# Gate matrix of a PEER layer: written as outer products by TensorE instead of scattered by GpSimd, with tiles 3 to 6 dense

## The chip, the cores and the metric

One core of a Trainium2 chip runs one decoder layer in float32. The metric is the device time of one execution in microseconds (us). TensorE is called PE here, VectorE DVE, ScalarE ACT, GpSimd POOL and SyncE SP; "PEld" is the weight load of PE.

## What is computed

The layer has a mixer (mLSTM heads beside stick-breaking attention), a cross-attention into 256 memory tokens, and a PEER feed-forward. Only the last part changes. For each of 1024 tokens, 8 heads pick 16 experts out of 16384; each expert is one row of `u` and one row of `v`, 1024 wide:

```
s_top, i_top = lax.top_k(s, PEER_TOPK)                    # per half of the product key
cand     = s_top[:, :, 0, :, None] + s_top[:, :, 1, None, :]
cand_idx = i_top[:, :, 0, :, None] * PEER_N_KEYS + i_top[:, :, 1, None, :]
best, pos = lax.top_k(cand..., PEER_TOPK)                 # 16 experts of a token and head
gates = softmax(best)
act = gelu(einsum('cd,ced->ce', xb, u[eb])) * gb          # eb: 128 experts of a token
y   = einsum('ce,ced->cd', act, v[eb])
```

An expert's number e is 128 i + p: i is one of 128 blocks of 128 experts, p the place in the block.

## The kernel before

The 1024 tokens are eight tiles of 128. The front of the kernel takes them in groups of (1, 2, 2, 1, 2) tiles: `part_a` (norm and projections), `mixers`, `post` (output projection, cross-attention, `route` with the expert scores) and `topk`, which finds a tile's 128 experts and gates per token. Work of the next group fills in beside the current one (`fill`). After `topk` there are two ways to compute the feed-forward:

- **Sparse tiles** (0, 1, 6, 7 before): `experts(tb)`. POOL fetches one row of `u` or `v` per token with an indirect DMA (L777, 512 KB), 128 of each per tile, into five buffers `uv`. DVE multiplies and sums a `u` row (L784) or adds a scaled `v` row to `y` (L790 for the first, L792). Four sparse tiles make 1024 gathers, and DVE has one instruction for each (a second, short one reads the accumulator).
- **Dense tiles** (2, 3, 4, 5 before): `dense()`. All 16384 experts are computed for the four tiles' N = 512 tokens, in 128 blocks. Block i needs a product h (24 matmuls, L850 in `hmat`), a GELU, a multiplication by block i of the gate matrix G (L876), a split into a high and a low half, and a product with `v` (24 matmuls, L896). Seven accumulators `y` stand in PSUM, the eighth, `y8`, is summed by DVE. `hmat` runs ahead of the gates by up to `ring` blocks.

G has 16384 rows and 512 columns and is zero but for 128 entries per token. It lies in HBM (`G_scr`). `zero_fill` (L116) first writes zeros in 256 DMAs on SP's queue, five after each weight load. Then, for each dense tile, `topk` issues 128 indirect DMAs on POOL (L748), each adding 128 gates of four bytes at places listed in `idx`. `dense` reads G block by block on SP's queue (L875).

The order on each engine is fixed when the program is built: a scheduler simulates the program and writes one list per engine. Each engine takes its own list strictly in order; an instruction that waits holds up all behind it. `dense` stands after the front in the program, and PE's part of it keeps that order.

Of the kernel before, what the change touches and what calls it, by code (L numbers as in the profile page):

```python
# [26 lines left out]
C_ID, C_TRI, C_MU, C_ST, C_IO, C_TK, C_SN, C_END = 0, 128, 256, 384, 512, 512 + NCAND, 520 + NCAND, 648 + NCAND  # L27


def constants():  # L30
    c = np.zeros((128, C_END), np.float32)
    p = np.arange(128)[:, None]
    f = np.arange(128)[None, :]
    c[:, C_ID:C_ID + 128] = p == f
    c[:, C_TRI:C_TRI + 128] = -(p >= f).astype(np.float32)
    c[:, C_MU:C_MU + 128] = np.where(p <= f, 0.0, NEG)
    c[:, C_ST:C_ST + 128] = p < f
    c[:, C_SN:C_SN + 128] = np.where(p < f, 0.0, NEG)
    c[:, C_IO:C_IO + NCAND] = np.arange(NCAND)[None, :]
    c[:, C_TK:C_TK + 8] = p + 128 * np.arange(8)[None, :]  # L40
    return c


class Layer:
# [65 lines left out]
    def zero_fill(self):  # L110
        z = self.fp.tile([128, 1, 128], F32, name="zero", bufs=1)
        self.nc.vector.memset(z, 0.0)
        n = self.zn
        g = self.G_d.rearrange("(c p n f) o -> c p n (f o)", p=128, n=n, f=128)
        for i in range(g.shape[0]):
            self.tc.keep_in_program_order(self.nc.sync.dma_start(g[i], z.to_broadcast([128, n, 128])))  # L116
            yield

# [30 lines left out]
    def ksmall(self, shape, name, bufs=2, dt=F32):  # L149
        return self.gp.tile(shape, dt, name=name, bufs=bufs)  # L150

    def xs(self):
        return self.fp.tile([128, D], F32, name="xs", bufs=3)
# [64 lines left out]
    def wload(self, w, c0):  # L218
        W = []
        for i in range(2):  # L220
            t = self.wtile([128, 4, 256])
            self.nc.sync.dma_start(t, w[512 * i:512 * i + 512, c0:c0 + 256].rearrange("(k p) n -> p k n", p=128))
            W += [t[:, k, :] for k in range(4)]
        for _ in range(self.zrate):
            next(self.zeros, None)
        return W
# [44 lines left out]
    def setup(self):  # L271
# [22 lines left out]
    def part_a(self, t0, nt):  # L294
# [13 lines left out]
        def ev_k(j, b):  # L308
            kc = self.mp.tile([128, T], F32, name="tk", bufs=2)
# [4 lines left out]
        def ev_v(t, b):  # L314
            vc = self.mp.tile([128, 512], F32, name="tk", bufs=2)
# [366 lines left out]
    def topk(self, tb, top, ti):  # L682
# [27 lines left out]
        pf = self.ksmall([128, NH, K16], "kpf", 1)  # L710
# [11 lines left out]
        self.idx[tb] = self.gp.tile([128, 128], I32, name="idx", bufs=4)  # L722
        self.gate[tb] = self.gp.tile([128, 128], F32, name="gate", bufs=4)
        exf = ex.rearrange("p h k -> p (h k)")
        if self.is_dense(tb):
            j = self.dl.index(tb)
            V.tensor_scalar(self.idx[tb], exf, float(128 * self.nd), self.c[:, C_TK + j:C_TK + j + 1],
                            op0=OP.mult, op1=OP.add)
        else:
            V.tensor_copy(self.idx[tb], exf)  # L730
        g = self.gate[tb].rearrange("p (h k) -> p h k", h=NH)
# [8 lines left out]
        rows = slice(128 * tb, 128 * tb + 128)  # L740
        self.dump("idx", self.idx[tb], lambda d: d[rows])
        self.dump("gate", self.gate[tb], lambda d: d[rows])
        if self.is_dense(tb):
            all_ = []
            for h in range(NH):
                same = []
                for k in range(16 * h, 16 * h + 16):
                    d = nc.gpsimd.indirect_dma_start(  # L748
                        out=self.G_d, out_offset=bass.IndirectOffsetOnAxis(ap=self.idx[tb][:, k:k + 1], axis=0),
                        in_=self.gate[tb][:, k:k + 1], in_offset=None, compute_op=OP.add)  # L750
                    for e in same:
                        self.tc.declare_no_dep(d.ins, e.ins, reason="one head's experts differ")
                    same.append(d)
                    if self.xt:
                        for e in self.scat[-self.xt:]:
                            self.tc.declare_no_dep(d.ins, e.ins, reason="tiles' columns differ")
                all_ += same
            self.scat += all_
# [56 lines left out]
    def dense_head(self):  # L815
# [4 lines left out]
        self.dh = f(tc.tile_pool(name="dh", bufs=1, side="right"))  # L820
# [36 lines left out]
    def dense(self):  # L857
# [3 lines left out]
        Gv = self.G_d.rearrange("(i p t) o -> i p (t o)", i=128, p=128)  # L861
# [8 lines left out]
        def gpart(i):  # L870
# [58 lines left out]
    def build(self, experts=True):  # L929
# [52 lines left out]
        for _ in self.zeros:  # L982
            pass
        self.front_ctx.close()
        tc = self.tc
        if self.nd:
            with tc.tile_pool(name="dp", bufs=1) as self.dp:
# [31 lines left out]
GROUPS = (1, 2, 2, 1, 2)  # L1019
# [18 lines left out]
```

## Time and profile before

| | us |
|---|---|
| median of 3 runs | 3686.97 |
| lowest and highest run | 3682.38, 3691.51 |
| the profiled execution: its span | 3682.8 |
| PE busy | 3024.6 (82%) |
| DVE busy | 2442.9 (66%) |
| POOL busy | 2135.7 (58%) |
| ACT busy | 1108.1 (30%) |

The span is the time of the one profiled execution, from its first instruction to its last. Shares of a whole span say little in this kernel, because its stages have different limits. A table by stretches of time shows for each stretch how long each engine was busy, the clock granted to PE (1.00 is 2.4 GHz), the busy share of the 16 DMA engines and the rate that they moved. A table of waits names who waited, for whom, for how long.

### The profile page before, as it was taken

The page shows a single profiled execution, that of the slowest core. Times are in us where ns is not written, and L with a number is a line of the kernel's source. Part 1 is how long each engine was busy: PE and PEld are TensorE (multiplying, and loading weights), DVE is VectorE, ACT ScalarE, POOL GpSimd, SP SyncE. Part 2 cuts the span into 40 slices and gives each one's busy share as a digit, 9 for nine tenths or more (in the row PEclk, how much of TensorE's full clock was granted, in tenths as well). Part 3 has the DMA queues.
Part 4 walks back from the last instruction along what each step waited for, and adds up shares of the span by engine and source line. Part 5 has one row for each costly group of instructions (what it writes and reads, how often), then busy time and mean ns, then how long its engine had stood idle before and what let it go on. Part 6 is the DMA issues. An engine that isn't in the chain of part 4 may idle for free.

```text
span 3682.8 us, 41986 instructions
## 1 busy us (share of the span) xinstructions
PE 3024.6 (82%) x14232; PEld 2481.8 (67%) x14232; DVE 2442.9 (66%) x5088; ACT 1108.1 (30%) x2236; POOL 2135.7 (58%) x1540
## 2 busy tenths in 40 slices
PE   8989999978975656664655655999999999999995
PEld 7777877767765545553444544777888887888884
DVE  0217767799953564435422265999888888888888
ACT  3423434323521212222222212233233233332323
POOL 0000545563368888888888887545555555555554
PEclk9999999989987878886787877999999999999997
DMA  9997999999895757664484656989999999999998
GB/s 295 281 322 239 350 334 343 364 316 330 284 304 130 212 139 182 181 154 103 78 216 104 178 118 179 351 309 344 344 342 343 346 339 327 347 340 345 337 334 297
DMA packets 572592, 992.49 MB, mean 269 GB/s; under 512 B 114392, under 2 KB 370520, under 8 KB 572376
## 3 DMA queue, kind: packets, MB, share of 16 engines
q0 software_dynamic: 221184, 537.23, 45.2%
q1 hardware_dynamic: 332144, 418.62, 34.9%
q10 hardware_dynamic: 19048, 33.96, 2.6%
q8 instruction: 112, 1.84, 0.2%
q14 instruction: 104, 0.85, 0.1%
HBM read 939.04 MB, written 50.59 MB: 269 GB/s over the span
## 4 chain that ended last, share of the span: by engine, by line
PE 25%; POOL 12%; issue 7%; DMA 5%; DVE 3%; ACT 1%; POOLq 0%; DVEq 0%; ACTq 0%
PE h L850 12%; PE y L896 11%; POOL G_scr L748 9%; POOL uv L777 4%; DMA uv<-v_in,idx 2%; PE h L896 2%; DMA G_scr<-gate,idx 1%; DMA uv<-u_in,idx 1%; DVE y L792 1%; DVE uv L784 0%; DVE vl L836 0%; DVE al L880 0%; ACT L123 0%; DVE y L899 0%; DVE ge L876 0%
## 5 line engine op out<-in xcount | busy, mean ns | idle before, releaser
L777 POOL DMA_INDIRECT uv<-u_in,idx x512 | 646.1, 1262 | 879.2 <-DVE idx L730 367.1
L748 POOL DMA_INDIRECT G_scr<-gate,idx x512 | 846.8, 1654 | 156.2 <-issue 151.3
L777 POOL DMA_INDIRECT uv<-v_in,idx x512 | 642.6, 1255 | 491.8 <-DVE act L784 224.3
L792 DVE SCALAR_TENSOR_TENSOR y<-uv,act,y 128x1024 f32<-128x1024 f32 x508 | 651.0, 1282 | 341.6 <-DMA uv<-v_in,idx 339.6
L784 DVE CUSTOM_DVE_ANT_0 uv<-uv,xf 128x1024 f32<-128x1024 f32 x512 | 623.8, 1221 | 367.8 <-DMA uv<-u_in,idx 367.0
L850 PE MATMUL h<-xs,uh 128*128 128x512 f32 x1968 | 619.5, 396 | 33.4 <-DVE y L899 15.3
L850 PEld LDWEIGHTS h<-xs,uh 128*128 128x128 f32 x1968 | 373.2, 190 | 120.0 <-DVE y L899 20.8
L238 PE MATMUL ps<-b,w 128*128 128x256 f32 (+1 forms) x2048 | 406.8, 356 | 32.3 <-ACT pq L670 18.3
L238 PEld LDWEIGHTS ps<-b,w 128*128 128x128 f32 x2048 | 347.7, 201 | 76.9 <-ACT pq L670 19.4
L850 PE MATMUL h<-xs,ul 128*128 128x512 f32 x984 | 388.7, 395 | 7.7 <-DVE ul L836 7.7
L896 PE MATMUL y<-vh,ah 128*128 128x512 f32 x896 | 352.3, 393 | 25.8 <-ACT ah L878 22.7
L834 ACT CAST uh<-ur 128x1024 fp32r<-128x1024 f32 x128 | 134.6, 1052 | 760.8 <-PE h L850 644.5
L896 PE MATMUL y<-vh,al 128*128 128x512 f32 x896 | 352.0, 393 | 1.0 <-DVE al L880 1.0
L896 PE MATMUL y<-vl,ah 128*128 128x512 f32 x896 | 350.3, 391 | 2.2 <-DVE vl L836 2.2
L238 PE MATMUL ps<-hT,w 128*128 128x256 f32 (+1 forms) x1280 | 254.8, 354 | 38.4 <-issue 16.9
L238 PEld LDWEIGHTS ps<-hT,w 128*128 128x128 f32 x1280 | 215.6, 201 | 68.7 <-issue 19.7
L850 PEld LDWEIGHTS h<-xs,ul 128*128 128x128 f32 x984 | 187.6, 191 | 48.4 <-DVE ul L836 8.1
L896 PEld LDWEIGHTS y<-vh,ah 128*128 128x128 f32 x896 | 169.3, 189 | 61.8 <-ACT ah L878 23.1
L250 PE MATMUL ps<-w,hT 128*128 128x256 f32 x768 | 184.8, 395 | 19.7 <-DMA w<-w_in_in 19.2
L836 DVE TENSOR_TENSOR ul<-ur,uh 128x1024 fp32r<-128x1024 f32 x128 | 156.6, 1223 | 63.7 <-ACT uh L834 63.7
L896 PEld LDWEIGHTS y<-vl,ah 128*128 128x128 f32 x896 | 169.2, 189 | 40.2 <-DVE vl L836 3.1
L896 PEld LDWEIGHTS y<-vh,al 128*128 128x128 f32 x896 | 169.1, 189 | 38.8 <-DVE al L880 1.7
(269 smaller groups left out, 4269.9 us busy)
## 6 DMA issues: line engine op xcount, KB each, us to landing
w<-w_in_in SPq DMA_DIRECT2D x140, 512.0 KB, 5.8
ur<-uT_in SPq DMA_DIRECT2D x128, 512.0 KB, 6.2
vr<-v_in SPq DMA_DIRECT2D x128, 512.0 KB, 5.9
w<-peer_wq_in SPq DMA_DIRECT2D x80, 512.0 KB, 5.4
G_scr<-zero SPq DMA_DIRECT2D x256, 128.0 KB, 4.9
G<-G_scr SPq DMA_DIRECT2D x128, 256.0 KB, 6.7
w<-w_out_in SPq DMA_DIRECT2D x40, 512.0 KB, 5.9
w<-wq_in SPq DMA_DIRECT2D x40, 512.0 KB, 5.8
```

The costliest lines, as they stand in the source:

```text
L238: nc.tensor.matmul(b[:, :T], W[k][:, 128 * (j % 2):128 * (j % 2) + 128], hT[:, k, :T], start=k == 0, stop=k == KC - 1)
L250: nc.tensor.matmul(b[:, 256 * q:256 * q + 256], hT[:, k, 128 * t:128 * t + 128], W[q][k], start=k == 0, stop=k == KC - 1)
L748: d = nc.gpsimd.indirect_dma_start(out=self.G_d, out_offset=bass.IndirectOffsetOnAxis(ap=self.idx[tb][:, k:k + 1], axis=0), in_=self.gate[ ...
L777: nc.gpsimd.indirect_dma_start(out=g, out_offset=None, in_=A[tbl], in_offset=bass.IndirectOffsetOnAxis(ap=self.idx[tb][:, s:s + 1], axis=0))
L784: V.tensor_tensor_reduce(u, u, xf, op0=OP.mult, op1=OP.add, scale=1.0, scalar=0.0, accum_out=act[:, s:s + 1])
L792: V.scalar_tensor_tensor(y, v, act[:, k:k + 1], y, op0=OP.mult, op1=OP.add)
L834: self.nc.scalar.copy(hi, src)
L836: self.nc.vector.tensor_sub(lo, src, hi.bitcast(F32))
L850: nc.tensor.matmul(h[:, :N], a[:, ks], self.xs_[:, x, k, :], start=n == 0, stop=n == 3 * KC - 1)
L896: nc.tensor.matmul(b, a[x][:, ts], v[w][:, qs], start=m == 0 and (j == 0 if acc else i == 0), stop=m == 2 and (j == 127 if acc else i == n ...
```

## The change

- `zero_fill`, `idx` of the dense tiles and the 512 indirect DMAs are gone. In their place `topk` calls `spread` for a dense tile. It transposes expert numbers and gates, so that a token is a column. For each token ACT writes |n - p| (L754) and, for two tokens at once, relu(1 - |n - p|) (L757): a one-hot of the place p of each of its 128 experts. DVE writes a one-hot of the block i times the gate (L755). PE multiplies the two (L760): a 128 x 128 slice of G. ACT copies four tokens' slices from PSUM in two halves (L763) and, after 16 tokens, stores two 512 KB pieces (L766) on its own queue. The staging buffers `gs` are two, one per half.
- `dense` reads G eight blocks at a time (2 MB, in runs of 512 bytes), 16 DMAs in all instead of 128.
- The groups are (1, 2, 2, 2, 1) and the dense tiles 3, 4, 5, 6, so 0, 1, 2 and 7 are sparse. Buffers are smaller: `ring` 5 for 12, `stb` 4 for 5, `wb` 5 for 6, `xs` 2 for 3, `tk` 1 for 2. Two pools wait tile by tile for their memory (`reuse_waits="tile"`).

On POOL, before, the 16 scatters of a head stand between gathers of tile 1 and later tiles:

```order
L777 DMA uv<-v_in,idx 128x1024 x33
L777 DMA uv<-u_in,idx 128x1024 x27
L748 DMA G_scr<-gate,idx 8388608x1 x16
L777 DMA uv<-u_in,idx 128x1024 x5
L748 DMA G_scr<-gate,idx 8388608x1 x16
```

Of such groups there are 32. Now POOL's list holds the 1024 gathers and nothing else.

On DVE, before, the first multiplication of dense gates (L876) stands amid gathers of tile 1 (L784, L792) and the choice of experts of the last group (L717 to L720); 441 gathers are consumed ahead of it:

```order
L720 TENSOR_REDUCE kex<-kA 128x8
L876 TENSOR_TENSOR ge<-ge,G 128x512 x2
L792 SCALAR_TENSOR_TENSOR y<-uv,act,y 128x1024
L717 TENSOR_TENSOR kA<-consts,kpf 128x400
L880 TENSOR_TENSOR al<-ge,ah 128x512 x2
L784 ISA uv,act<-uv,xf 128x1024
```

In the changed kernel the same multiplication (L885) comes when the experts of tile 7, the last, are chosen (L707 to L717):

```order
L705 TENSOR_TENSOR kA<-consts,kpos 128x400
L707 TENSOR_TENSOR kA<-kA,kcidx 128x400
L708 TENSOR_REDUCE kex<-kA 128x8
L717 CAST idx<-kex 128x128
L875 MEMSET y_13675 128x512
L885 TENSOR_TENSOR ge<-ge,G 128x512 x4
L844 TENSOR_TENSOR ul<-ur,uh 128x1024
L889 TENSOR_TENSOR al<-ge,ah 128x512
L885 TENSOR_TENSOR ge<-ge,G 128x512
L792 ISA uv,act<-uv,xf 128x1024
```

All 768 gathers of tiles 0, 1 and 2 are consumed ahead of it, and none of tile 7. Between the last of the 768 and this place DVE's list holds what tiles 5 and 6 need for their slices of G, and tile 7's `post` and `topk`.

On PE, at the end of the slices of tiles 5 and 6 (L760), the list now goes:

```order
L858 MATMUL h<-xs,ul 128x512
L734 MATMUL pt<-consts,kex 128x128
L735 MATMUL pt<-consts,kbest 128x128
L760 MATMUL pt<-ab 128x128 x126
L760 MATMUL pt<-ab 128x128 x128
L188 MATMUL pt<-consts,xs 128x128 x4
L760 MATMUL pt<-ab 128x128 x2
L228 MATMUL ps<-b_12893,w 128x128 x6
```

L228 on `b_12893` is the query projection of tile 7's cross-attention: it and all behind it, up to the dense blocks, come after the last slices. Tiles 3 and 4 have such a row of slices too, earlier. Four of the 128 products h stand ahead of the first product with `v`; before, there were twelve.

The core of the diff:

```diff
-GROUPS = (1, 2, 2, 1, 2)
+GROUPS = (1, 2, 2, 2, 1)
-        Layer(ctx, tc, A, out[0], S, GROUPS, dense=(2, 3, 4, 5), uvb=5, stb=5, wb=6, ..., ring=12, ...
+        Layer(ctx, tc, A, out[0], S, GROUPS, dense=(3, 4, 5, 6), uvb=5, stb=4, wb=5, ..., ring=5, ...
...
-        if self.is_dense(tb):
-            all_ = []
-            for h in range(NH):
-                same = []
-                for k in range(16 * h, 16 * h + 16):
-                    d = nc.gpsimd.indirect_dma_start(
-                        out=self.G_d, out_offset=bass.IndirectOffsetOnAxis(ap=self.idx[tb][:, k:k + 1], axis=0),
-                        in_=self.gate[tb][:, k:k + 1], in_offset=None, compute_op=OP.add)
...
+        if dense:
+            yield from self.spread(self.dl.index(tb), exf, gate)
+
+    def spread(self, j, exf, gate):
...
+        for c in range(128 // TC):
+            st = [self.ksmall([128, 64, TC], "gs", 2) for _ in range(2)]
+            for q in range(TC // 4):
+                b = self.bank("pt")
+                for m in range(2):
+                    ab = self.ksmall([128, 2, 2, 128], "ab", 2)
+                    for i in range(2):
+                        t = TC * c + 4 * q + 2 * m + i
+                        nc.scalar.activation(ab[:, 0, i, :], iota, AF.Abs, bias=sl[:, 0, t:t + 1])
+                        V.tensor_scalar(ab[:, 1, i, :], iota, sl[:, 1, t:t + 1], sl[:, 2, t:t + 1], op0=OP.is_equal,
+                                        op1=OP.mult)
+                    nc.scalar.activation(ab[:, 0], ab[:, 0], AF.Relu, scale=-1.0, bias=self.one)
+                    for i in range(2):
+                        o = 128 * (2 * m + i)
+                        nc.tensor.matmul(b[:, o:o + 128], ab[:, 0, i, :], ab[:, 1, i, :], start=True, stop=True)
+                bv = b.rearrange("p (t h i) -> p t h i", t=4, h=2)
+                for h in range(2):
+                    nc.scalar.copy(st[h][:, :, 4 * q:4 * q + 4].rearrange("p i t -> p t i"), bv[:, :, h, :])
+                yield
+            for h in range(2):
+                nc.scalar.dma_start(self.G_d[:, h, (128 // TC) * j + c], st[h])
...
-            G = dp.tile([128, N], F32, name="G", bufs=self.gb)
-            nc.sync.dma_start(G, Gv[i])
-            V.tensor_mul(ge, ge, G)
+            if i % NB == 0:
+                self.Gt = dp.tile([128, N // TC, NB, TC], F32, name="G", bufs=self.gb)
+                nc.sync.dma_start(self.Gt, self.G_d[:, i // 64, :, i % 64:i % 64 + NB, :])
+            gv = ge.rearrange("p (c t) -> p c t", t=TC)
+            V.tensor_mul(gv, gv, self.Gt[:, :, i % NB, :])
```

## Rows read from the trace of the kernel before

**Rows 1.** By stretches: length; busy per engine (instructions); PE clock, DMA share, GB/s.

```profile
0.00:365.00 365.00, 322.12 (x1829) 277.95 (x1830) 109.35 (x455) 123.17 (x351) 0.20 (x4) 0.97 0.94 287
365.00:990.00 625.00, 566.97 (x2891) 464.99 (x2890) 509.10 (x1213) 249.93 (x605) 306.64 (x257) 0.95 0.94 334
990.00:1055.00 65.00, 55.92 (x274) 44.49 (x273) 55.64 (x118) 22.10 (x55) 28.96 (x26) 0.92 0.86 299
1055.00:2277.00 1222.00, 729.74 (x3386) 590.16 (x3384) 544.83 (x1768) 284.12 (x652) 1014.53 (x676) 0.78 0.62 153
2510.00:2760.00 250.00, 248.48 (x1089) 203.87 (x1088) 220.25 (x286) 76.04 (x96) 145.43 (x108) 1.00 0.95 345
```

**Rows 2.** Waits in 1055 to 2270 us: who and for whom, total us, times, longest.

```profile
POOL G_scr L748 <- issue: 151.3, 496, 0.3
DVE y L792 <- DMA uv<-v_in,idx: 279.1, 33, 23.2
DVE uv L784 <- DMA uv<-u_in,idx: 272.6, 39, 25.0
```

**Rows 3.** Groups by line on POOL: count, busy us, mean ns, idle before them.

```profile
L748 POOL DMA_INDIRECT G_scr<-gate,idx x512 | 846.8, 1654 | 156.2 <-issue 151.3 <-DMA G_scr<-gate,idx 4.6 <-DVE kA L686 0.3
```

**Rows 4.** Dense lines: first and last start; busy by stretch; pieces of the chain.

```profile
L896 PE MATMUL y<-vh,ah x896: 388/389/796, 2277.1 to 3648.0; 128*128 128x512 f32 x180
...
1880.00:2277.00 397.00, 80.31 (x288) 60.67 (x288) 0.78 0.59 143
...
2515.28 5.47 PE h L850 x24
```

**Rows 5.** DMA queues in 365 to 990 us, then in 0 to 365: packets, MB, share.

```profile
q0 software_dynamic: 36864, 134.23, 58.8%
q1 hardware_dynamic: 64120, 66.64, 31.7%
...
q1 hardware_dynamic: 133522, 98.94, 89.8%
```

**Rows 6.** DMA queues of the whole span, and issues: count, KB each, us to landing.

```profile
q1 hardware_dynamic: 332144, 418.62, 34.9%
q10 hardware_dynamic: 19048, 33.96, 2.6%
...
x_scr<-xa ACTq DMA_DIRECT2D x3, 1024.0 KB, 7.2
```

**Rows 7.** DVE in order of time near 950 us: start, length.

```profile
949.29 1.28 DVE L792 SCALAR_TENSOR_TENSOR y<-uv,act,y 128x1024 f32<-128x1024 f32 x1
950.49 0.69 DVE L533 SCALAR_TENSOR_TENSOR sq<-pz,sq 128x512 f32<-128x512 f32 x1
```

**Rows 8.** Groups by line and shape, rows like the new instructions on ACT and DVE.

```profile
L128 ACT ACTIVATE ta<-ta 128x128 f32<-128x128 f32 x16 | 4.9, 308 | 30.3 <-DVE ta L354 30.2
L129 ACT ACTIVATE ta<-ta,one 128x128 f32<-128x128 f32 x16 | 6.4, 401 | 0.2
L128 ACT ACTIVATE ta<-ta 128x256 f32<-128x256 f32 x24 | 9.9, 412 | 27.0 <-DVE ta L354 27.0
L129 ACT ACTIVATE ta<-ta,one 128x256 f32<-128x256 f32 x24 | 12.1, 505 | 0.2
L658 ACT COPY ta<-pt 128x256 f32<-128x256 f32 x64 | 23.1, 374 | 189.8 <-DVE kti L665 94.2 <-PE pt L655 91.3 <-DVE kti L662 3.9
L424 DVE TENSOR_SCALAR mnM<-mM 4x128 f32<-4x128 f32 x8 | 1.7, 213 | 0.2
```

**Rows 9.** Tile 0 alone, 0 to 420 us: query projection, scores, choice of experts.

```profile
L584 ACT ACTIVATE b<-ps x8: 277/278/278, 201.6 to 214.7; 128x128 f32<-128x128 f32 x8
...
L658 ACT COPY ta<-pt x8: 372/375/378, 268.6 to 312.1; 128x256 f32<-128x256 f32 x8
...
L720 DVE TENSOR_REDUCE kex<-kA x16: 559/569/570, 325.2 to 366.1; 128x8 f32<-128x400 f32 x16
```

More of the change, by code (lines that the diff above doesn't have):

```diff
@@ L108, in row_bcast @@
         self.nc.scalar.dma_start(dst, bass.AP(tensor=r.tensor, offset=r.offset, ap=[[0, 128], [1, D]]))
[L110 to L117, printed above, removed]
     def is_dense(self, tb):
@@ L149, in ksmall @@
     def ksmall(self, shape, name, bufs=2, dt=F32):
[L150 removed]
+        return self.fp.tile(shape, dt, name=name, bufs=bufs)
     def xs(self):
[L153 removed]
+        return self.fp.tile([128, D], F32, name="xs", bufs=2)
     def b8(self, shape):
@@ L223, in wload @@
             W += [t[:, k, :] for k in range(4)]
-        for _ in range(self.zrate):
-            next(self.zeros, None)
         return W
@@ L308, in ev_k @@
         def ev_k(j, b):
-            kc = self.mp.tile([128, T], F32, name="tk", bufs=2)
+            kc = self.mp.tile([128, T], F32, name="tk", bufs=1)
             nc.scalar.copy(kc, b)
@@ L314, in ev_v @@
         def ev_v(t, b):
-            vc = self.mp.tile([128, 512], F32, name="tk", bufs=2)
+            vc = self.mp.tile([128, 512], F32, name="tk", bufs=1)
             nc.scalar.copy(vc, b)
@@ L721, in topk @@
             yield
-        self.idx[tb] = self.gp.tile([128, 128], I32, name="idx", bufs=4)
-        self.gate[tb] = self.gp.tile([128, 128], F32, name="gate", bufs=4)
         exf = ex.rearrange("p h k -> p (h k)")
-        if self.is_dense(tb):
-            j = self.dl.index(tb)
-            V.tensor_scalar(self.idx[tb], exf, float(128 * self.nd), self.c[:, C_TK + j:C_TK + j + 1],
-                            op0=OP.mult, op1=OP.add)
-        else:
+        dense = self.is_dense(tb)
+        if dense:
+            gate = self.ksmall([128, 128], "kbest", 1)
+        else:
+            gate = self.gate[tb] = self.gp.tile([128, 128], F32, name="gate", bufs=4)
+            self.idx[tb] = self.gp.tile([128, 128], I32, name="idx", bufs=4)
             V.tensor_copy(self.idx[tb], exf)
-        g = self.gate[tb].rearrange("p (h k) -> p h k", h=NH)
+        g = gate.rearrange("p (h k) -> p h k", h=NH)
         be = self.ksmall([128, NH, K16], "kcand", 1)
@@ L986, in build @@
         if self.nd:
-            with tc.tile_pool(name="dp", bufs=1) as self.dp:
+            with tc.tile_pool(name="dp", bufs=1, reuse_waits="tile") as self.dp:
                 with tc.tile_pool(name="yps", bufs=1, space=PSUM) as self.yps:
@@ L1032 @@
     with tile.TileContext(nc, schedule_with_timeline_sim=True) as tc, ExitStack() as ctx:
-        Layer(ctx, tc, A, out[0], S, GROUPS, dense=(2, 3, 4, 5), uvb=5, stb=5, wb=6, ra=(1, 0.6, 0.0), flr=(1, 3, 0),
-              ring=12, lead=2, fill0=True, fills=(2, 5), cap=10, zrate=5, banks=(2, 2, 3, 1), off=500, tg=("pt", "pt"),
+        Layer(ctx, tc, A, out[0], S, GROUPS, dense=(3, 4, 5, 6), uvb=5, stb=4, wb=5, ra=(1, 0.6, 0.0), flr=(1, 3, 0),
+              ring=5, lead=2, fill0=True, fills=(2, 5), cap=10, zrate=5, banks=(2, 2, 3, 1), off=500, tg=("pt", "pt"),
               vrb=2, gb=2, yw=2).build()
```

46 lines of the change are left out of this document (23 added, 23 removed).

## The prediction, made before the changed kernel had run

> **What bounds the kernel now.** I read the table by stretches first [rows 1], then the waits of its weakest stretch [rows 2, 3], then the dense lines [rows 4]. Three stretches are full: up to 365 us PE is busy 88% of the time, from 365 to 990 us PE 91%, DVE 81% and the DMA engines 94%, and in the dense stage PE 99% and DMA 95%. One is not: from 1055 to 2277 us PE, DVE and DMA are busy 60%, 45% and 62%. POOL is the limit there: 1014.5 us busy in 1222, and between its instructions mostly 0.3 us of issue (496 times before a scatter). DVE waits 552 us in that stretch for gathers that stand behind scatters in POOL's list, and PE with it; the granted clock is 0.78, between its levels of 2.4 and 1.2 GHz. 512 scatters of 1.654 us and 0.3 us of issue are 1000 us of POOL. The first product with v begins at 2277.1 us; from there PE runs dense blocks nearly without a gap until 3648.8, and 34 us of last sums and stores follow.
>
> So the time is: start of the dense products (call it y0), plus dense, plus 34. What matters is who sets y0 once POOL no longer does.
>
> **The change, part by part.** The sum is made against the profiled execution, 3682.8 us, 4 below the median.
>
> *Scatters and zero fill.* The 1000 us of POOL go. Does y0 move by that much? In the new order all 768 gathers of tiles 0, 1 and 2 are consumed on DVE ahead of the first gate product, where 441 were. Tile 0's 256 fall into 365 to 990 us in both kernels (134.2 MB there at 0.524 MB each [rows 5]), so 512 replace 185 behind 990 us. The zero fill leaves SP's queue and 33.5 MB leave the DMA engines before 365 us; PE, 88% busy there, is held by its own chains, so I take 0, at most 20. A weight buffer fewer is hidden by the same stretch's free DMA time, and later by PE's slack.
>
> *Stage 2, the 512 gathers of tiles 1 and 2, from 990 us.* Three prices.
> DMA: 512 x 0.524 MB = 268 MB. Of the 418.6 MB of SP and ACT loads [rows 6], 33.5 are zeros, 33.5 are G, 136 dense operands, so 215 are the front's; 98.9 - 33.5 + 66.6 = 132 passed before 990 us [rows 5], 83 remain, 17 of them for tile 7's last weights: 66. Slices of G for tiles 3 and 4 are 17 MB, other stores some 13. Sum 364 MB. At 334 GB/s, the rate of 365 to 990 us, 1090 us; at 345, the best long stretch, 1055.
> DVE: a gather takes 1.2 us start to start [rows 7]: 614 us. The other work of the front is 600 us busy from 990 to 2277 less 185 x 1.2 and some 25 of dense operands, about 355, plus 40 for the last choice of experts, which now also precedes y0. Slices cost 512 multiplications at about 0.2 us, the nearest row being 0.213 for 4 x 128 [rows 8]: 100. Of 1110 us some 190 belong to stage 3, so 920 here, if DVE never idles.
> Pace of 365 to 990 us: 256 gathers in 625 us, 2.44 each: 1250.
> I take 1090, the DMA price, with 920 and 1250 as ends. PE isn't among them: it has less than half of that time's work left. Tiles 3 and 4's slices lie in this stage beside some 120 gathers (250 us by the DMA price); they occupy ACT alone for about as long, and cost nothing only while those gathers take that time.
>
> *Stage 3, from the last of the 768 gathers to y0.* It has no gathers to consume, and its parts are serial, since ACT, DVE and PE each have them in this order. (a) The rest of tile 5's experts, 25 us (15 steps of three DVE operations). (b) Slices of tiles 5 and 6: 64 times four tokens. ACT per four: four Abs of 128, two Relu of 256, two copies of 256. By rows without a bias operand 4 x 0.308 + 2 x 0.412 + 2 x 0.374 = 2.8 us, by rows with one 4 x 0.401 + 2 x 0.505 + 0.75 = 3.4 [rows 8]: 179 or 215 us. To that comes a wait: the two `gs` buffers go out together after 16 tokens, and the next copy waits until the store has landed. The nearest row, a store of twice the size from ACT's queue, takes 7.2 us [rows 6]; I count 2 to 5 us uncovered, 16 times: 32 to 80. Ends 180 and 300; I take 250, since both operands here are with bias and the store does stand in the way. (c) Tile 7's query projection to its scores: tile 0 alone took 312.1 - 201.6 = 110 us for this [rows 9], under a full DMA; 105. (d) Its choice of experts, 312.1 to 366.1: 54 with other work between, 45. (e) First product and split, 5. Sum 430, ends 340 and 520.
>
> y0 = 990 + 1090 + 430 = 2510, where it was 2277.
>
> *Dense.* 24 products take 5.47 us [rows 4]. Before, 288 matmuls, 12 products h, were done ahead of y0; with `ring` 5 only 4 are: 252 x 5.47 = 1378 us remain instead of 244 x 5.47 = 1335. The stage took 1371.7, so it lost 37; I take 25, since only 256 gathers remain beside it (583 before), so that the second half has DMA and DVE to spare, which no one uses. G comes in runs of 512 bytes. The zero fill wrote such: 98.9 MB took 89.8% of 365 us, 328 us; less 65.4 MB at 336 GB/s (66.6 MB in 31.7% of 625 us) leaves 133 us for 33.5 MB, 252 GB/s. G would so take 133 us of DMA instead of 100, half of it in the full part: 0 to 17 us, I take 0.
>
> Sum: 2510 + 1378 + 25 + 34 = 3947; on the median's scale 3950, 7% above 3687.
>
> *A rule weighed.* DMA moved 345 GB/s over 250 us at a share of 0.95 [rows 1]. The Trainium skill (DMA: Bandwidth & Descriptors, Where 436 GB/s comes from) gives about 358 GB/s as a core's HBM limit and quotes 425 measured for one core with the other of its pair idle. With 425, stage 2 would be down to DVE's 920 and the time at 3780, still slower; no long stretch here shows more than 345.
>
> **Rivals.**
> *PE sets the front's pace (faster).* If DVE did not have to consume gathers ahead of the dense stage, PE's work decides: 786 us busy from 990 to 2277 at a clock near 0.78 is about 620 at full clock, less 66 for early products h, plus 512 slices at about 0.3 (0.25 to 0.4), some 150: 700, at 91% busy 770. y0 = 1760, time 3200. For it: POOL's stretch is plainly the weak one. The Trainium skill (Trace Analysis, Optimization Strategy) would have the most contended engine of each regime relieved first, and adds that regimes may gain by being interleaved: the first half leads here, the second speaks against putting 768 gathers in front. Against it: DVE's list is fixed. It decides if stage 2 takes under 400 us, for which DVE alone needs 920.
> *DVE never idles (level).* Stage 2 at 920 and stage 3 at 340: y0 = 2250, time 3690. For it, DVE at 100% near 950 us. Against it, 81% over 625 us, and a stage 3 whose DVE work fills less than half of its time.
> *The slices stall (slower yet).* If each four tokens cost 6 us, because ACT, PE and DVE wait for each other with two `ab` and two PSUM buffers at the lower clock, (b) is 385 and the slices of tiles 3 and 4 outlast their gathers by about 130: 4210.
> *The change does not do what it says* is not among them: POOL's list has no scatters.
>
> **How the numbers follow.** Forecast 3950, chance 0.73, own range 3740 to 4100: stage 2 from 920 to 1250 and stage 3 from 340 to 520 give 3690 to 4200 at both extremes at once, which I narrow by about 50 at the low and 100 at the high end. Slices stall 0.11, level 0.04, PE sets the pace 0.12. 3740 to 4100 leaves out the fast case, the level one and part of the slow one, about 0.2 with the tails. Within 0.3% (11 us, about what can be told from no change): 0.04. Faster 0.12, slower 0.84.
>
> **What the new profile would show.** No POOL busy time beyond 1024 gathers. From 990 us DMA near 0.94 and DVE near 0.85, PE under 0.6 with the clock down in the slices. The last of the 768 gathers consumed near 2080; then some 430 us without them, ACT solid with L754, L757, L763, and waits of ACT for stores of `gs`. First L905 near 2510. Dense blocks 10.95 us each, DMA share well under 0.9 in their second half. I am wrong if L905 starts before 2250 or if gathers go faster than one in 1.9 us over the stage.

## The result and the profile after

The changed kernel takes 3953.3 us (median of 4 runs, 3951.3 to 3968.8), the kernel before 3689.1 beside it (3682.4 to 3691.5): 1.073 times as long, 95% interval 1.071 to 1.075. Forecast were 3950 us and slower. The profiled execution spans 3967.1 us; all terms below are of that one.

The page of the changed kernel: busy time by engine, then busy tenths, granted clock and DMA share in 40 slices of 99 us.

```profile
PE 3307.5 (83%) x15264; PEld 2696.9 (68%) x15264; DVE 2601.4 (66%) x5619; ACT 1490.2 (38%) x3256; POOL 1252.2 (32%) x1028
...
PE   8999899887798415467986567699999999999998
...
DVE  0238766899969989885679732788888843333333
ACT  3425343431442217672532686132232232222223
POOL 0002544454644664563441000155555500000000
PEclk9999999898998655558997557899999999999999
DMA  6677999999898887898998113699999943434432
```

The same by stretches, cut where the work changes (columns as in [rows 1]):

```profile
365.00:943.00 578.00, 497.43 (x2349) 401.89 (x2348) 458.96 (x1035) 208.66 (x512) 278.22 (x243) 0.92 0.94 332
943.00:1483.00 540.00, 350.29 (x1568) 265.84 (x1568) 462.33 (x1117) 151.88 (x324) 307.74 (x245) 0.81 0.90 311
1483.00:1757.00 274.00, 147.77 (x516) 118.35 (x517) 243.33 (x548) 206.24 (x522) 147.85 (x123) 0.50 0.85 296
1757.00:2151.00 394.00, 333.73 (x1681) 275.29 (x1680) 282.45 (x702) 132.31 (x342) 164.49 (x145) 0.91 0.94 329
2151.00:2207.00 56.00, 27.90 (x74) 18.00 (x74) 46.28 (x131) 18.48 (x33) 0.00 (x0) 0.62 0.27 86
2207.00:2429.00 222.00, 147.08 (x538) 119.46 (x538) 107.19 (x361) 192.50 (x515) 0.00 (x0) 0.51 0.18 72
2429.00:2558.00 129.00, 85.75 (x579) 77.80 (x577) 65.17 (x280) 32.44 (x88) 2.56 (x2) 0.86 0.59 182
2558.00:3180.00 622.00, 611.43 (x2647) 496.55 (x2648) 523.20 (x644) 187.20 (x238) 337.12 (x254) 0.99 0.95 336
3180.00:3949.00 769.00, 769.00 (x3379) 633.82 (x3377) 282.61 (x320) 223.26 (x298) 0.00 (x0) 1.00 0.38 115
```

The 512 scatters, 847 us of POOL and 151 of issue [rows 2, 3], are gone, and with them the 552 us of DVE's waits behind scatters. What stands there instead: 943 to 1483 us is tile 1's gathers and the front of tiles 3 and 4; 1483 to 1757 the slices of tiles 3 and 4, beside gathers; 1757 to 2151 the front of tiles 5 and 6, beside the last gathers of tile 2; 2151 to 2207 the choice of experts of tile 5; 2207 to 2429 the slices of tiles 5 and 6, with DMA at 0.18 and POOL idle; 2429 to 2558 tile 7. In both rows of slices PE's granted clock is 0.50 to 0.51, its lower level of 1.2 GHz; between the products PE waits, most of the time for ACT (123 us for L757 over the four tiles). Then the dense stage: DMA 0.95 and DVE 84% while tile 7's gathers last, 0.38 and 37% afterwards. The second half of the dense stage has room for 256 gathers more, which the front has done already, at 2.36 us each.

The first product with `v`, y0, and the last sums of tile 2, the third sparse tile (DVE in order of time):

```profile
L905 PE MATMUL y<-vh,ah x896: 389/389/796, 2558.4 to 3948.5; 128*128 128x512 f32 x180
...
2149.92 0.68 DVE L814 TENSOR_TENSOR uv<-uv,y 128x512 f32<-128x512 f32 x1
```

y0 was 2277.1 [rows 4], so the front became 281 us longer, where 1000 us of POOL went.

In the table stage 2 runs from tile 0's last gather to tile 2's, and stage 3 from there to y0:

| term (us) | forecast | measured |
|---|---|---|
| tile 0's last gather (stage 2 begins) | 990 | 943 |
| stage 2, 512 gathers of tiles 1 and 2 | 1090 | 1207 |
| stage 3, from there to y0 | 430 | 408 |
| y0 | 2510 | 2558 |
| dense | 1403 | 1391 |
| tail | 34 | 18 |
| span | 3947 | 3967 |

### The profile page after: what moved, and what is told of

It is laid out like the page before. It is cut to its first block, busy times and chain, and to the rows that moved or that the text cites. A ratio compares the mean times of both kernels' runs of the same rounds, so it can differ in the third digit from the quotient of the medians.

```text
span 3967.1 us, 45127 instructions
## 1 busy us (share of the span) xinstructions
PE 3307.5 (83%) x15264; PEld 2696.9 (68%) x15264; DVE 2601.4 (66%) x5619; ACT 1490.2 (38%) x3256; POOL 1252.2 (32%) x1028
## 5 line engine op out<-in xcount | busy, mean ns | idle before, releaser
L785 POOL DMA_INDIRECT uv<-v_in,idx x512 | 613.7, 1199 | 572.9 <-DVE act L792 243.7
L792 DVE CUSTOM_DVE_ANT_0 uv<-uv,xf 128x1024 f32<-128x1024 f32 x512 | 622.1, 1218 | 105.3 <-DMA uv<-u_in,idx 104.4
L858 PE MATMUL h<-xs,uh 128*128 128x512 f32 x2032 | 638.3, 395 | 42.7 <-ACT uh L842 18.3
L858 PEld LDWEIGHTS h<-xs,uh 128*128 128x128 f32 x2032 | 384.0, 190 | 136.1 <-ACT uh L842 18.7
L760 PE MATMUL pt<-ab 128*128 128x128 f32 x1024 | 290.6, 452 | 207.3 <-ACT ab L757 123.3
L760 PEld LDWEIGHTS pt<-ab 128*128 128x128 f32 x1024 | 234.0, 323 | 264.3 <-ACT ab L757 192.3
L228 PE MATMUL ps<-b,w 128*128 128x256 f32 (+1 forms) x2048 | 391.5, 346 | 16.9 <-DMA w<-wq_in 12.3
L858 PE MATMUL h<-xs,ul 128*128 128x512 f32 x1016 | 399.5, 393 | 1.0 <-DVE ul L844 1.0
L228 PEld LDWEIGHTS ps<-b,w 128*128 128x128 f32 x2048 | 333.3, 194 | 55.9 <-DMA w<-wq_in 13.1
L228 PE MATMUL ps<-hT,w 128*128 128x256 f32 (+1 forms) x1280 | 253.9, 353 | 23.6 <-DMA w<-w_in_in 15.3
L228 PEld LDWEIGHTS ps<-hT,w 128*128 128x128 f32 x1280 | 214.5, 201 | 55.1 <-DMA w<-w_in_in 13.9
L755 DVE TENSOR_SCALAR ab<-consts,ksl 128x128 f32<-128x128 f32 x512 | 153.8, 346 | 116.4 <-PE pt L760 100.5
L754 ACT ACTIVATE ab<-consts,ksl 128x128 f32<-128x128 f32 x512 | 172.8, 390 | 77.8 <-DVE ksl L742 55.4
```

Source lines behind the costliest of these rows:

```text
L228: nc.tensor.matmul(b[:, :T], W[k][:, 128 * (j % 2):128 * (j % 2) + 128], hT[:, k, :T], start=k == 0, stop=k == KC - 1)
L754: nc.scalar.activation(ab[:, 0, i, :], iota, AF.Abs, bias=sl[:, 0, t:t + 1])
L755: V.tensor_scalar(ab[:, 1, i, :], iota, sl[:, 1, t:t + 1], sl[:, 2, t:t + 1], op0=OP.is_equal, op1=OP.mult)
L760: nc.tensor.matmul(b[:, o:o + 128], ab[:, 0, i, :], ab[:, 1, i, :], start=True, stop=True)
L785: nc.gpsimd.indirect_dma_start(out=g, out_offset=None, in_=A[tbl], in_offset=bass.IndirectOffsetOnAxis(ap=self.idx[tb][:, s:s + 1], axis=0))
L792: V.tensor_tensor_reduce(u, u, xf, op0=OP.mult, op1=OP.add, scale=1.0, scalar=0.0, accum_out=act[:, s:s + 1])
```

## Experiments

Where no ratio stands, a time is a single one, beside which I give the time of y0 and of the ends of stages in that run's trace; y0 is what to compare, since about 1391 us of dense and 18 of tail follow it in most of them. The four runs of the changed kernel lie 17 us apart, and the profiled one is the longest of them, so a difference of less than some 20 us between single runs shows nothing by itself. One warning holds for all: the scheduler writes DVE's list anew for each kernel, so an edit also changes how many gathers stand ahead of a given step. I count them in each trace.

**The two parts apart.** The order alone, scatters kept:

```diff
-GROUPS = (1, 2, 2, 1, 2)          # kernel before
+GROUPS = (1, 2, 2, 2, 1)
-        ... dense=(2, 3, 4, 5), ...
+        ... dense=(3, 4, 5, 6), ...
```

> The kernel before (scatters on POOL) with the changed kernel's order alone: tiles 3 to 6 dense, groups (1,2,2,2,1). On DVE some 580 gathers now stand ahead of the first gate product, 441 before. My theory (what stands ahead of the first product with v, y0, sets the time; the order alone costs): POOL still has 512 scatters and about 140 gathers more ahead of y0, at 1.2 + 0.3 us each 210 us, so y0 near 2490 and 3850 to 3900 us. Rival (the outer products are the loss, the order is harmless): 3690, as before.

Measured: 3989.6 us, 1.082 times before (1.079 to 1.085), y0 2623. The order alone costs, and by more than I had counted. The stretch from just before the first scatter (1408 us) to y0, POOL's group and DVE's waits in it:

```profile
1390.00:2622.00 1232.00, 423.26 (x2071) 348.98 (x2071) 464.81 (x1265) 166.82 (x392) 1017.51 (x674) 0.66 0.54 124
...
L748 POOL DMA_INDIRECT G_scr<-gate,idx x512 | 849.5, 1659 | 157.3 <-issue 152.2 <-DMA G_scr<-gate,idx 4.2 <-DVE sq L533 1.0
...
DVE uv L784 <- DMA uv<-u_in,idx: 398.2, 48, 30.8
DVE y L792 <- DMA uv<-v_in,idx: 319.9, 37, 30.2
```

The 512 scatters take what they took in [rows 3], but they begin 350 us later, because the first dense pair is tiles 3 and 4. POOL is the bound again, from a later start.

The outer products alone, order of before:

```diff
-GROUPS = (1, 2, 2, 2, 1)          # changed kernel
+GROUPS = (1, 2, 2, 1, 2)
-        ... dense=(3, 4, 5, 6), ...
+        ... dense=(2, 3, 4, 5), ...
```

> The changed kernel with the order of before alone put back: tiles 2 to 5 dense, groups (1,2,2,1,2). On DVE some 590 gathers stand ahead of the first gate product instead of 768. My theory: 178 gathers fewer at 2.35 us are 418 us less of the gathering stage, and one tile's slices more lie where nothing is gathered (+131 us); y0 near 2230 (2000 to 2300) and about 3640 us (3400 to 3700), at or under the kernel before. Rival (the outer products themselves are the loss): about 3950, as the changed kernel.

Measured: 4135.5 us, 1.121 times before (1.118 to 1.123), y0 2691. Theory and rival both missed: each part alone is worse than both together (1.082 and 1.121 against 1.073). Stretches: tile 5's front, then that of tiles 6 and 7, then what comes ahead of y0; and a wait in the last.

```profile
1796.00:2096.00 300.00, 255.56 (x1411) 208.49 (x1409) 108.08 (x396) 100.12 (x237) 0.00 (x0) 0.92 0.46 142
2204.00:2515.00 311.00, 266.69 (x1254) 217.14 (x1252) 103.11 (x449) 119.11 (x268) 0.00 (x0) 0.93 0.33 104
2515.00:2691.00 176.00, 7.76 (x24) 5.91 (x24) 158.30 (x332) 9.46 (x14) 112.71 (x84) 0.52 0.82 274
...
POOL uv L785 <- DVE kA L674: 1037.4, 1, 1037.4
```

I had priced the front by its gathers. From 1526 us, when tile 1's gathers end, to 2515 there is not one gather, POOL waits 1037 us for the next indices, and the front takes 990 us nevertheless: PE 85% busy in its fronts, and three tiles' slices between them (1575 to 1796 and 2096 to 2204), in which PE does nothing else. Then some 80 gathers of tile 6, which DVE's list has ahead of the first gate product, hold PE for 176 us. So the front has a chain of its own, which takes this long without any gather. (In the changed kernel the same three tiles' fronts, with four tiles' slices and 271 gathers among them, take 1075 us, from 1483 to 2558.)

**What the slices cost.** `spread` without one-hots, products and copies:

```diff
-                    for i in range(2): ... nc.scalar.activation(...), V.tensor_scalar(...)
-                    ... nc.tensor.matmul(...)
-                for h in range(2):
-                    nc.scalar.copy(...)
+        gz = self.ksmall([128, 64, TC], "gs", 1)    # zeroed once per tile, stored 16 x 2 times
```

> The changed kernel without the one-hots, their products and their copies: each dense tile stores a zeroed tile 16 times two, so the stores and all else stay. My theory: the slices of tiles 5 and 6, 263 us in the trace, lie alone on the path, those of tiles 3 and 4 beside gathers: 3650 to 3700. Rival (the slices lie beside DMA-paced work anyway): above 3900. If tiles 3 and 4's also stand on the path: below 3600.

Measured: 3735.2 us, y0 2325. Tile 2's last gather comes at 2165 (2150 with slices), and stage 3 is 160 us instead of 408: the slices of tiles 5 and 6 were worth 248 there. (From first product to last they take 219 us in the changed kernel, not the 263 of the expectation.) Those of tiles 3 and 4 did not move the end of stage 2; but tile 0 ended at 1008 in this list, 65 later, and stage 2 took 1157, so up to 50 us of it may have been theirs. The time lies 35 us above the range; the late start may be the reason.

**What paces stage 2.** For tiles 1 and 2, half of DVE's work, half of the bytes, and both:

```diff
+                    w = 512 if tb in (1, 2) else D
-                    V.tensor_tensor_reduce(u, u, xf, ...
+                    V.tensor_tensor_reduce(u[:, :w], u[:, :w], xf[:, :w], ...
...
+            rows = A[tbl] if w == D else A[tbl].rearrange("r (o n) -> (r o) n", n=w)
-            nc.gpsimd.indirect_dma_start(out=g, out_offset=None, in_=A[tbl],
+            nc.gpsimd.indirect_dma_start(out=g[:, :w], out_offset=None, in_=rows,
```

> The changed kernel, but for tiles 1 and 2 DVE's two operations per gathered pair of rows run over 512 of 1024 columns (the rest is left out); the gathers stay whole. 508 operations lose about 0.6 us each, 300 us of DVE. My theory (the DMA engines set the pace of the 512 gathers, 1205 us at a share of 0.90): the stage loses at most 80 us, 3870 to 3960 in all. Rival (DVE sets it): 300 us less, about 3650.

> The changed kernel, but the gathers of tiles 1 and 2 fetch 512 of 1024 numbers per row (134 MB less, wrong rows), while DVE still works over 1024: the operation on u as two of 512, that on v over the same half twice, which adds about 0.15 us 256 times. After the run with half of DVE's work (its stage of gathers still took 1178 us, 27 less, while y0 came 169 us earlier) my theory is that DMA paces the gathers and DVE paces the front's chain between them. DMA price of the stage then (375 - 134) MB at 311 GB/s = 775 us, DVE's list about 1050: the stage falls by 100 to 150 us and y0 by as much: 3800 to 3860. Rival (DVE's list and the ring of five buffers pace the gathers, bytes don't matter): stage within 30 us of 1205, total above 3920.

> The changed kernel with half rows gathered for tiles 1 and 2 and DVE's operations on them over 512 columns only (half of the bytes and half of DVE's work of these gathers left out). My theory (DMA and DVE share the pace, 0.90 and 0.85 busy): with both relieved the stage falls to what the front itself takes, 750 to 950 us, and the total to 3450 to 3650. Rival (a fixed cost per gather: POOL's 1.2 us, the ring): the stage stays above 1100 and the total near 3800, as with DVE's half alone.

Measured: 3801.0 us with DVE's half (y0 2389), 3949.8 with half of the bytes (y0 2541), 3867.2 with both (y0 2459). None came out as expected, and the traces say why. From tile 0's end to the first slices: the changed kernel (its stretch stands above), then DVE's half, half of the bytes, both.

```profile
941.00:1336.00 395.00, 341.80 (x1569) 262.25 (x1570) 291.67 (x1016) 148.14 (x321) 186.40 (x177) 0.90 0.93 331
```

```profile
942.00:1468.00 526.00, 360.28 (x1579) 274.26 (x1577) 491.23 (x1389) 155.59 (x333) 300.67 (x259) 0.81 0.67 206
...
1782.00:2190.00 408.00, 350.70 (x1755) 287.53 (x1754) 264.44 (x805) 148.69 (x375) 105.43 (x87) 0.91 0.61 199
...
1951.02 1.29 DVE L820 TENSOR_TENSOR uv<-uv,y 128x512 f32<-128x512 f32 x2 [0.16 <-DMA uv<-x_scr]
```

```profile
944.00:1416.00 472.00, 375.05 (x1569) 285.98 (x1570) 366.21 (x1184) 155.05 (x333) 309.07 (x285) 0.81 0.78 245
...
1778.45 0.69 DVE L818 TENSOR_TENSOR uv<-uv,y 128x512 f32<-128x512 f32 x1
```

DVE's groups in the first stretch, changed kernel and DVE's half (count | busy, mean ns | idle before):

```profile
L792 DVE CUSTOM_DVE_ANT_0 uv<-uv,xf 128x1024 f32<-128x1024 f32 x128 | 155.7, 1217 | 33.1 <-DMA uv<-u_in,idx 32.9
L800 DVE SCALAR_TENSOR_TENSOR y<-uv,act,y 128x1024 f32<-128x1024 f32 x112 | 142.9, 1276 | 6.9 <-DMA uv<-v_in,idx 6.9
```

```profile
L793 DVE CUSTOM_DVE_ANT_0 uv<-uv,xf 128x512 f32<-128x512 f32 x102 | 69.6, 684 | 10.0 <-DMA uv<-u_in,idx 9.8
L802 DVE SCALAR_TENSOR_TENSOR y<-uv,act,y 128x512 f32<-128x512 f32 x69 | 51.5, 746 | 12.9 <-DMA uv<-v_in,idx 12.9
```

The changed kernel consumes 240 gathers in these 540 us, 2.25 us each; with DVE's half it is 171 in 395, 2.31 each. So DVE's relief did not make a gather faster; the new list merely has 69 gathers fewer ahead of the first slices, and these came 147 us earlier. Over the whole stage 2 the same: 1178 us instead of 1207. Half of the bytes does make gathers faster: all 512 are done at 1952 us, 199 earlier, now with DVE 93% busy (491 of 526). With both halves they are done at 1779 us, 835 after tile 0's end, within the 750 to 950 that I had expected. So DMA paces the gathers, with DVE's list next in line.

But y0 did not follow. Half of the bytes moved it by 18 us, no more than runs of one kernel differ, and both halves by 99, though there all gathers were done 372 us earlier, and 326 us without any stand ahead of the second slices (1779 to 2105). With half of the bytes part of that is the run's own doing: its extra work on DVE made the first slices 314 us long instead of 274. The rest goes with PE: from the end of the first slices to the start of the second, that is for the front of tiles 5 and 6 and the choice of tile 5, it is 450 us in the changed kernel, 408 with half of the bytes and 409 with both halves, PE busy for 348 to 362 of them. With both halves the list also put more gathers ahead of the first slices (279, 1.69 us each), which is why it is worse than DVE's half alone.

**Which engine sets a slice.** Row one-hots by a comparison on DVE:

```diff
-                        nc.scalar.activation(ab[:, 0, i, :], iota, AF.Abs, bias=sl[:, 0, t:t + 1])
-                    nc.scalar.activation(ab[:, 0], ab[:, 0], AF.Relu, scale=-1.0, bias=self.one)
+                    V.tensor_tensor(ab[:, 0], <iota for two tokens>, <two tokens' indices>, op=OP.is_equal)
```

> The changed kernel with the row one-hots built by DVE (one comparison over 2 x 128 per two tokens, about 0.4 us) instead of two Abs and one Relu on ACT: ACT per four tokens falls from 4.0 to 1.2 us, DVE rises from 1.2 to 2.0. My theory (ACT's list sets the slices): four tokens take 2.2 to 2.6 us, the slices of tiles 5 and 6 140 to 170 instead of 263, total 3840 to 3880. Rival (PE at 1.2 GHz and the hand-over between the engines set them): under 30 us less, above 3920.

Measured: 3993.4 us, y0 2584: the time lies where the rival had it, above 3920, but not for its reason. The slices of tiles 5 and 6 take 162 us instead of 219, so ACT's list did set them; but those of tiles 3 and 4 now take 374 instead of 274 (the front behind them, with its choice, 435 for 450):

```profile
1479.00:1853.00 374.00, 151.06 (x519) 119.40 (x519) 338.32 (x744) 79.54 (x150) 223.70 (x168) 0.50 0.82 280
1853.00:2288.00 435.00, 357.32 (x1751) 291.18 (x1751) 276.43 (x765) 148.26 (x365) 113.61 (x100) 0.88 0.74 255
2288.00:2450.00 162.00, 128.77 (x519) 103.44 (x520) 140.97 (x486) 68.18 (x131) 0.00 (x0) 0.64 0.24 98
```

Where gathers stand on DVE, it is 90% busy and the one-hots wait in its list; where none do, the edit saves 57 us.

**The fill.** Its writes put back, into a buffer that nobody reads:

```diff
+        self.Z_d = nc.dram_tensor("Z_scr", (128 * 128 * 128 * 4, 1), F32, kind="Internal").ap()
...
+        for _ in range(self.zrate):
+            next(self.zeros, None)
```

> The changed kernel with the removed fill's 33.5 MB of writes put back on SP's queue at the same places, into a buffer that nobody reads. My prediction priced the fill's removal at 0 (at most 20 us); tile 0's last gather came at 942 us in the changed kernel and at 990 in the one before. Theory (the fill costs nothing, the 45 us come from the new order): 3945 to 3965, tile 0's end within 15 us of 942. Rival (the fill held the first stage back): tile 0's end at 970 to 990 and 20 to 45 us more in all.

Measured: 3983.7 us; by spans 3981.9 against 3967.1, 15 more. Tile 0's gathers end at 982 us instead of 943, y0 is 2574 instead of 2558. In the first 365 us PE is busy 310 us, 337 without the fill, and DMA 0.93 instead of 0.68:

```profile
0.00:365.00 365.00, 309.71 (x1780) 264.23 (x1781) 99.03 (x429) 115.45 (x336) 0.20 (x4) 0.99 0.93 280
```

By the end of stage 1 the rival holds: the fill costs about 40 us there. Other runs agree: with the fill tile 0 ends at 980 us (the order alone) and 993 (the kernel before); without it at 926 to 948 in ten of eleven kernels and at 1008 in the one without slices. At y0 16 us are left and in the whole span 15, less than the rival had and no more than runs of one kernel differ.

**Gathers of tile 2 behind y0, and slices among other work.** Held gathers:

```diff
+            if i == 0:
+                ...
+                V.tensor_scalar(self.zero1, ge[:, :1], 0.0, None, op0=OP.mult)
...
+        if tb in (2, 7):
+            late = gp.tile([128, 128], I32, name="idx", bufs=4)
+            V.tensor_scalar(late, self.idx[tb], self.zero1, None, op0=OP.add)
+            self.idx[tb] = late
```

> The changed kernel, but the 512 gathers of tiles 2 and 7 wait for the first gate product (their indices get a zero added that is computed from it), so only tiles 0 and 1 stand ahead of y0 on DVE (512 gathers instead of 768). Half of the bytes moved y0 by 18 us only, half of DVE's work by 169. My theory: y0 is the end of the front's own chain, and DVE's list, in which the gathers stand, paces that chain. First slices again near 1483, front of tiles 5 and 6 in 300 us instead of 450 (as with the old order, 2204 to 2510 for two tiles), y0 2370 to 2420, dense 1391 + 0 to 40 with 512 gathers beside it: 3770 to 3860. Rival (tile 2's gathers lie in gaps of the front): y0 within 40 of 2558, above 3910.

Measured: 3896.2 us, y0 2464, 94 less; I had expected 140 to 190. The slices of tiles 3 and 4, beside the last 15 gathers of tile 1, then the front of tiles 5 and 6, without any:

```profile
1483.00:1713.00 230.00, 145.76 (x521) 118.16 (x522) 129.53 (x389) 195.18 (x523) 11.64 (x12) 0.50 0.29 106
1713.00:2111.00 398.00, 347.10 (x1750) 284.41 (x1748) 153.34 (x619) 140.81 (x360) 0.00 (x0) 0.91 0.45 142
```

The first get 44 us shorter (230 for 274), the second 52 (398 for 450, the choice of tile 5 included): 96 together, which is what y0 gained. I had expected 300 us for the second, the length of a front in the run with the old order, but that was one of a single tile, or of two with part of their work done earlier. Here PE is 87% busy and DVE 39%: without gathers, PE is by far the busiest engine of this stretch.

Slices written among the next group's steps:

```diff
             for _ in mix:
...
-                next(fl, None)
-            drain(fl)
+                for _ in range(2):
+                    next(fl, None)
...
             for _ in self.post(*starts[i]):
...
+                for _ in range(2):
+                    next(fl, None)
+            drain(fl)
...
-                drain(self.flush(self.flr[1]))
+                self.pending.sort(key=lambda q: self.is_dense(q[0]))
+                drain(self.flush(sum(not self.is_dense(q[0]) for q in self.pending)))
```

The last lines leave only the sparse tiles' choices in the block behind `post`.

> The changed kernel, but the choices of experts and the slices of tiles 3, 4 and of 5, 6 are written among the next group's steps (two pieces per step) and no longer in one block between the groups. My theory (the slices stand alone on ACT while PE waits at 1.2 GHz; 219 us for tiles 5 and 6): they go beside tile 7's front, and y0 falls by 150 to 250, held by the 512 gathers, which end near 2150 with 130 us behind them: 3690 to 3800. Rival (DVE's list holds all of it, so order within the front gives nothing back): above 3900.

Measured: 3800.8 us, 1.031 times before (1.028 to 1.034), y0 2400: 158 us less, as expected but at the low end, so that the time is just above the range given. The stretches of the two pairs' slices, with what now stands among them:

```profile
1486.00:1898.00 412.00, 309.62 (x1535) 252.53 (x1533) 327.60 (x711) 285.97 (x743) 181.09 (x157) 0.81 0.87 308
...
2076.00:2362.00 286.00, 188.19 (x929) 161.87 (x930) 192.50 (x616) 212.96 (x582) 48.91 (x46) 0.67 0.54 191
```

From the first slice to the last it is 877 us instead of 944, and from the last slice to y0 37 instead of 131, since tile 7's front now stands beside the slices of tiles 5 and 6: the second is the larger part of the gain.

> Both edits: tile 2's gathers behind the first gate product and the slices written among the next group's steps. My theory: the two gains add, since one takes work out of DVE's list and the other takes ACT's block off the chain: y0 2150 to 2250, 3560 to 3680, at or under the kernel before. Rival (one bound behind both): no better than the better of the two alone.

Measured: 3708.6 us, 1.0056 times before (1.0039 to 1.0073), y0 2275. The gains add (94 + 158 = 252; 283 measured), since they come from different pieces of one chain; but y0 stayed 25 above the range I gave, dense grew to 1416 with 512 gathers beside it, and the sum ends just above the kernel before.

> The held and interleaved kernel (3709 us, y0 2275) with the row one-hots built by DVE as in the run where that alone cost 26 us of y0. There DVE's list was full of gathers; here, from 1560 us to y0, no gather stands on DVE (it is busy 25 to 60 of 70 us) and ACT is busy 47 to 61 of 70. My theory (which engine is the scarce one decides what the same edit is worth): y0 falls by 50 to 120, to 2155 to 2225, total 3590 to 3660, under the kernel before. Rival (the hand-over between engines or PE at 1.2 GHz paces the slices): within 30 us of 3709.

Measured: 3603.3 us, 0.976 times before (0.974 to 0.979), y0 2170: 105 us less than without the comparison on DVE, which cost 26 in the changed kernel. Time and y0 lie in the ranges expected, and it is the fastest of all. The stretch of tiles 3 and 4's slices with the front of tiles 5 and 6 beside them, held and interleaved, and then with the comparison on DVE:

```profile
1484.00:1844.00 360.00, 298.44 (x1543) 245.50 (x1541) 173.43 (x485) 275.81 (x742) 12.75 (x13) 0.83 0.43 146
```

```profile
1480.00:1800.00 320.00, 285.43 (x1595) 240.06 (x1594) 213.39 (x626) 164.51 (x381) 13.81 (x14) 0.93 0.51 174
```

From the start of the first slices to that of the second it is now 444 us (1483 to 1927), where the changed kernel took 724 (1483 to 2207), and PE is busy for 88% of it (389.5 us) at a clock of 0.93.

## Why the prediction was right, and where its steps were not

The sign was right for the reason given: POOL's 1000 us left, and gathers, slices and tile 7 took their place ahead of y0. That the time came within 3 us is luck: the terms of the table are off by 47, 117, 22, 12 and 16 us with both signs, and they add up to a span 20 above the sum, in an execution that was itself 16 above the median. Step by step:

- *Zero fill, 0, at most 20.* Mis-sized for the end of stage 1, where the run with the fill put back shows 39 us; the 15 at the end of that run are within what I allowed. That PE was 88% busy in that stretch did not mean that nothing could hold it up: without the fill it was 92%.
- *Stage 2 by its DMA price, 1090.* The mechanism held, the rate did not. The bytes were right: 311, 296 and 329 GB/s over 540, 274 and 394 us are 379 MB, against 364 plus the 16 MB that 47 us of earlier start add. The mean is 314 GB/s instead of 334, which makes the stage 1207. DVE's floor of 920 was near: with half of the bytes the 512 gathers took 1010 us, 48 of them that run's own extra work on DVE (two operations of 683 ns and a second sum for one of 1217).
- *"PE isn't among them."* This is the step that failed, and the sum hid it. I gave PE less than half of stage 2 as work; it was busy for 832 of the 1208 us, 69%, in part at the lower clock. And I compared PE's work with the whole stage. But PE has nothing else to do in the 274 us of slices, and the front of tiles 5 and 6 does not begin before they end; without gathers beside them, these slices still take 230 us and that front with its choice 398. So from the start of the first slices to that of the second PE's chain takes 628 us even then, where the path by the last gather took 724 (1483 to 2207). "Last gather plus stage 3" did set y0, but nothing that makes tile 2's gathers faster could have given more than about 96 us there, which is what holding them back gave.
- *Slices of tiles 3 and 4, nothing.* The last gather ends at 2165 without any slices and at 2150 with them, but from a stage 2 that began 65 us later, so that up to 50 us stay open. The slices do lie on PE's chain: interleaving them and those of tiles 5 and 6 gave 158 us.
- *Stage 3, 430.* Measured 408, as the pieces of DVE's order of time show (last slice of tile 6, first step of tile 7's choice):

```profile
2424.18 0.60 DVE L755 TENSOR_SCALAR ab<-consts,ksl 128x128 f32<-128x128 f32 x2 [1.57 <-PE pt L760]
...
2513.47 0.32 DVE L684 TENSOR_TENSOR kcand<-ktop 128x64 f32<-128x64 f32 x2
```

  (a) 56 for 25; (b) 222 for 250; (c) 84 for 105; (d) and (e) 45 for 50. In (b) two errors cancelled. The groups in 2207 to 2429 us:

```profile
L754 ACT ACTIVATE ab<-consts,ksl 128x128 f32<-128x128 f32 x252 | 84.6, 390 | 2.1 <-PE pt L760 1.3 <-DVE ksl L742 0.7
L755 DVE TENSOR_SCALAR ab<-consts,ksl 128x128 f32<-128x128 f32 x256 | 76.9, 342 | 107.9 <-PE pt L760 93.2 <-ACT ab L757 13.2 <-ACT ab L754 0.9
L763 ACT COPY gs<-pt 128x256 f32<-128x256 f32 x128 | 67.5, 604 | 23.3 <-PE pt L760 23.3
L757 ACT ACTIVATE ab<-ab,one 128x256 f32<-128x256 f32 x128 | 62.7, 502 | 3.5 <-ACT ab L754 1.3
```

  Abs and Relu came as [rows 8] had them with a bias. The copy took 604 ns where the row of the same size took 374; it writes every sixteenth number, which may be the reason, but no run tried it otherwise. The wait for `gs` stores, which I counted at 32 to 80 us, is absent from this stretch; over all four tiles it was 20.4 us in 14 waits, the store landing in 3.8 us rather than 7.2. ACT's three groups add up to 215 us (192.5 without their overlaps) in 222, so ACT is nearly solid, as forecast.
- *Dense 1403, tail 34.* 1391 and 18: the dense stage lost 13 us instead of 25, and the tail was half because no gather is left for DVE at the end (the last ended at 3176; before, at 3673, behind the last product). G in runs of 512 bytes cost nothing that can be seen.
- *The rule weighed.* The long full stretches of the changed kernel moved 329 to 336 GB/s at DMA shares of 0.94 to 0.95. That no long stretch shows more than 345 was not quite so; the kernel before has one with 352:

```profile
425.00:725.00 300.00, 284.69 (x1410) 232.33 (x1408) 218.03 (x380) 123.47 (x294) 152.82 (x128) 0.97 0.97 352
```

  The Trainium skill (DMA: Bandwidth & Descriptors, Where 436 GB/s comes from) gives about 358 GB/s as a core's HBM limit and quotes 425 as measured. Nothing here supports 425, and the long stretches do not contradict 358. Stretches of 100 us show more, up to 386 (625 to 725 us, before), but with a DMA share of 1.02, so they are too short to be taken at their word. Stage 2 at 920 us did not come about.
- *Rivals.* PE setting the front's pace (3200) was far off, since 512 gathers do stand ahead; but PE's chain was nearer than I had it, as the third point says: PE was busy for 68% of the time from 943 us to y0, not under 60%. The Trainium skill (Perfetto Trace Analysis, Optimization Strategy) says that regimes may gain by being interleaved; the runs agree, with 158 us for interleaving ACT's regime with PE's. "The slices stall" did not happen: 3.4 us per four tokens (219 / 64).

What stays open: how much of the 2.25 us per gather from 943 to 1483 us would go if fewer stood there, since no run held tile 1's back; and how far the list that the scheduler happened to write moves each single time: tile 0's end lies at 926 to 948 us in ten kernels without the fill whose first stage I did not touch, and at 1008 in an eleventh. No run put the larger buffers back either. From 943 to 2558 us PE waits 33 us for weights, where it waited 12 from 990 to 2277 before, so by these waits the weight buffer that is gone is worth some 20 of the 281 us at most; the price of `ring` stands in the sum (43 us of the dense stage), and the other buffers were not priced.

## What to carry to other kernels

Removing a bound engine's work pays only as much as the next chain allows, and that chain must be added up piece by piece in program order: comparing an engine's total work with a stage's total length misses that it may be shut out of part of the stage. When a step moves to another engine, look which engine is scarce in that very stretch: the same comparison on DVE made the slices beside gathers 100 us longer and those without 57 us shorter, 26 us lost in all, and gave 105 in the kernel where hardly a gather stood among them. A step that leaves the other engines idle (here ACT's slices) belongs among their work, not between it, and work that a later stage has room for (tile 2's gathers) should be held for it: holding them and interleaving the slices gave 94 and 158 us of y0 by themselves and 283 together.

## What the runs showed of the hardware that I had not expected

- A copy on ACT of 128x256 that wrote every sixteenth number took 604 ns; the one of before, which wrote them in a row, 374 [rows 8].
- A product of 128x128 by 128x128 in f32 took 450 ns at the granted clock of 0.50 to 0.51 that PE had while it waited for ACT between products; written among other PE work, in the last experiment, the clock was 0.93 and the mean 317 ns:

```profile
L762 PE MATMUL pt<-ab 128*128 128x128 f32 x512 | 88.5, 317 | 22.5 <-DVE ab L757 10.6 <-ACT gs L765 9.9 <-DVE mden L481 0.7
```

- The 33.5 MB of the fill, in a stretch whose DMA share was 0.93 with them and 0.68 without, went with 27 us less of PE's busy time in 365.
